# Hybrid mLSTM and sparse-attention block: the opening by token tiles with the first half of mv, and another rate for top-k

## The chip, the core and the metric

The kernel runs on one NeuronCore of a Trainium2 chip. The metric is the time of one execution on the device in microseconds (us). One profiled execution, with a trace of every engine, stands beside the timed runs. TensorE (PE in the rows) multiplies, VectorE (DVE), ScalarE (ACT) and GpSimd (POOL) work on rows, SyncE (SP) issues most transfers.

## What is computed

One decoder block on 512 tokens of width 1024, all in float32: an RMS norm, one wide input projection, an mLSTM group and a sparse attention group side by side, an output projection, and a gated per-layer embedding with a final norm. Cut to what matters here:

```python
u = rmsnorm(h, norm_in[i])
proj = u @ w_in[i]
(m_q, m_k, m_v, m_o, m_z, m_if, a_q, a_k, a_v, a_z,
 ix_q, ix_k, ix_w) = jnp.split(proj, SPLIT_POINTS, axis=-1)
qk = jax.nn.silu(causal_dwconv(jnp.concatenate([m_q, m_k], axis=-1), conv_w[i]))
...
hm = mlstm_chunkwise(mq, mk, m_v, log_i, log_f)
hm = jax.nn.sigmoid(m_o) * norm(hm) * jax.nn.silu(m_z)
# sparse attention: score[t, s] = sum_h ix_w[t, h] * relu(ix_q[t, h] . ix_k[s]), causal,
# each token attends to its 128 best keys, softmax with a relative bias
ha = dsa_attention(a_q, a_k, a_v, ix_q, ix_k, ix_w, rel_bias) * jax.nn.silu(a_z)
h = h + jnp.concatenate([hm, ha], axis=-1) @ w_out[i]
h = h + (p[i] @ w_ple[i]) * jax.nn.sigmoid(h @ w_ple_gate[i])
return rmsnorm(h, norm_final)
```

## The kernel before

Every large product is made in three passes of a reduced float32: each operand is split into a high part (wh, uH: a copy by ScalarE) and a low part (wl, uL: a subtraction by VectorE, or by GpSimd for the slabs in `POOLP`), and TensorE adds high times high, high times low and low times high. u, the normalised input, lies in SBUF with its 1024 features over the partitions, in 8 pieces of 128 (kt), as uH and uL. Weights come in slabs of 512 KB (raw, 3 buffers; wh and wl, 4 each), in the order of a plan; `piece()` gives the next slab and has the later ones loaded and split.

The projection goes in blocks of 512 columns: `dense_fm` gives features by tokens, `dense_tm` tokens by features. Both use four PSUM banks (tag mm), and the next block may begin in a bank when the one before it has been evacuated. Four more banks (tag x) serve transposes and small products. The order is: opening with iq (the indexer's queries) and misc (its keys, its weights and the gates), mq, mk, mv in two halves, then o and z, then mLSTM woven with the second o and z, av and two pairs of aqk, then attention woven with the rest, the output projection and the gate.

Beside the blocks runs a queue of small steps, `back`: the 24 score steps of the indexer, the gate sequences, the conv of the eight mq and mk pieces, and 48 top-k steps (16 rounds of MAX and MATCH_REPLACE for three token tiles), later `split_mix`, the split of the mLSTM's result (mixH, mixL). `beat()`, called twice per slab row of a block, gives the queue one credit; a step costs COST_SC, COST_CV, COST_TK or COST_MX. So the costs set how densely the steps are spread over the blocks. What is left of top-k is issued ahead of attention. From the order of the program and its own model of time the scheduler sets each engine's order; the opening alone is written out by hand (`manual_schedule`).

In the opening before, the eight x transfers come first. For each token tile ScalarE squares the two halves of x (`junk`), the sum goes to the power of -0.5 on GpSimd; TensorE transposes x by pieces of 128 features and spreads the four rows of factors over the partitions (`rps`, then `rB`). Per kt VectorE then scales 512 tokens at once (`scaled`), ScalarE and VectorE split (`high`, `low`), one half slab of iq weights is split (`weights`), and TensorE adds that kt's products to the four iq banks. misc follows from a transfer of its own (`mraw`). The rest of the text calls the eviction of mv by its rows: v (high, ScalarE; low, VectorE); that of z: sz. The relative bias goes out to memory and back: `tdram` is written and `tz` read, both issued from ScalarE's queue, so ScalarE stands until the write has landed.

Of the kernel before, what the change touches and what calls it, by code (L numbers as in the profile page):

```python
# [32 lines left out]
COST_SC, COST_CV, COST_TK, COST_MX, RATE = 1.3, 1.5, 1.5, 3.0, 1.4  # L33
# [14 lines left out]
def block_kernel(ctx: ExitStack, tc: tile.TileContext, x, p, w_in, b_gate, conv_w, w_out, norm_in,  # L48
# [94 lines left out]
    def split(k):  # L143
        raw = loaded.pop(k)
        nk, n = raw.shape[1:]
        h = wp.tile([P, KP * S], F32R, tag="wh", bufs=NW, name="wh")[:, 0:nk * n].rearrange("p (k n) -> p k n", n=n)
# [3 lines left out]
        ready[k] = h, l  # L150

# [109 lines left out]

# [41 lines left out]
    def weights(kt):

        q, k = kt // KP, kt % KP
        if k == 0:
            iqw[q] = [wp.tile([P, KP, S], F32R, tag=t, bufs=NW, name=t) for t in ("wh", "wl")]
        h, l = iqw[q]
        A.activation(h[:, k, :], loaded[q][:, k, :], AF.Copy)
        (G if kt in POOLW else V).tensor_tensor(l[:, k, :], loaded[q][:, k, :], f(h)[:, k, :], OP.subtract)  # L310

    us = {}

    def scaled(kt):
        us[kt] = tmp("u")
        V.scalar_tensor_tensor(us[kt], xt[kt], g_in(kt), rB, op0=OP.mult, op1=OP.mult)

    def high(kt):
        A.activation(uH[:, kt, :], us[kt], AF.Copy)

    def low(kt):
        V.tensor_tensor(uL[:, kt, :], us.pop(kt), f(uH[:, kt, :]), OP.subtract)

    load(0)
    load(1)
    EN = mybir.EngineType
    with tc.manual_schedule(engines={EN.PE, EN.DVE, EN.Activation, EN.Pool}):

        for kt in range(4):
            xt[kt] = mm_bank(f"xt{kt}")  # L330
        vps = x_bank("vps")
        xt[4], xt[5] = x_bank("xt4"), x_bank("xt5")
        rps = x_bank("rps")
        for i in range(NT):
            if i == 3:
                T.transpose(vps[:, 0:48], vrows, ident[0:48, 0:48])
                V.tensor_copy(vcols[:, 0:48], vps[:, 0:48])
                V.tensor_scalar(vcols[:, 48:56], vcols[:, 8:16], 0.25, None, op0=OP.mult)
            for kt in range(4):
                turn(kt, i)  # L340
            for c in range(2):
                junk = tmp("junk")
                A.activation(junk, xs[i][c], AF.Square, scale=D ** -0.5, accum_out=ss[:, i, c:c + 1])
            V.scalar_tensor_tensor(ss[:, i, 2:3], ss[:, i, 0:1], EPS, ss[:, i, 1:2], op0=OP.add, op1=OP.add)
            G.tensor_tensor(ss[:, i, 3:4], ss[:, i, 2:3], neghalf[:, 0:1], OP.pow)
        for i in range(3):
            spread(i)
        weights(0)
        turn(4, 0)
        turn(4, 1)  # L350
        turn(4, 2)
        spread(3)
        turn(4, 3)
        for i in range(NT):
            turn(5, i)
        rB = tmp("rB")
        A.activation(rB, rps, AF.Copy)
        xt[6] = x_bank("xt6")
        for i in range(NT):
            turn(6, i)  # L360
        for kt in range(KT):
            if kt == 0:
                scaled(0)
                scaled(1)
            high(kt)
            low(kt)
            if kt < KT - 1:
                weights(kt + 1)
            if kt < KT - 2:
                scaled(kt + 2)  # L370
            if kt == 0:
                mraw = wp.tile([P, KT, 80], F32, tag="raw", bufs=NR, name="mraw")
                nc.sync.dma_start(mraw[:, :, 0:72], wv[:, :, C_IK:C_IK + 72])
                nc.sync.dma_start(mraw[:, :, 72:80], wv[:, :, C_IF:C_IF + 8])
                nc.sync.dma_start(gb[72:76, 0:1], b_gate[0, 0:4].rearrange("(h o) -> h o", o=1))
# [604 lines left out]
```

## Time and profile before

| | us |
|---|---|
| median of 3 runs | 527.07 (526.15 to 527.16) |
| the profiled execution's own time | 526.94 |
| its span, first to last instruction | 524.9 |
| TensorE busy | 498.6 (95%) |
| VectorE busy | 349.3 (67%) |
| ScalarE busy | 259.8 (49%) |
| GpSimd busy | 81.3 (15%) |

The span and what lies around it (2.0 us) make the execution's time. A busy TensorE is not TensorE at its peak: records of products overlap, and the distance from one start to the next is what one costs. The idle time of an engine counts only where the engine that ends last waits for it; so the waits of TensorE and the chain of work are read before any sum of busy time.

### The profile page before, as it was taken

What the parts mean: (1) busy time and instruction counts of PE and PEld (TensorE: products, weight loads), DVE (VectorE), ACT (ScalarE), POOL (GpSimd) and SP (SyncE); (2) the same over time, 40 slices, a digit from 0 to 9 for tenths busy, and PEclk for the clock granted to TensorE, in tenths of its full rate; (3) what the DMA queues carried; (4) which work ended last, traced back from release to release, by engine and by line L of the source; (5) the groups of instructions that cost most, each with busy time, mean ns of one, the idle gap of its engine ahead of it and who ended that gap; (6) DMA issues with size and microseconds to landing.
All of it is one profiled execution on the core that took longest, in us unless ns stands there. A gap on an engine that the chain in (4) does not pass through costs nothing.

```text
span 524.9 us, 6706 instructions
## 1 busy us (share of the span) xinstructions
PE 498.6 (95%) x2370; PEld 409.3 (78%) x2370; DVE 349.3 (67%) x718; ACT 259.8 (49%) x518; POOL 81.3 (15%) x110
## 2 busy tenths in 40 slices
PE   4999999894999999999999999999999999999994
PEld 3887878683878888888888787888878888888884
DVE  0945287999999827355745759979887441452744
ACT  5636183763132425465545658767875321232533
POOL 4501022231111322310101012111111000000011
PEclk9999999997999999999999999999999999999998
DMA  8352557322223224223422312121123443213012
GB/s 264 108 181 84 104 87 172 117 82 81 81 85 116 82 81 140 77 92 112 131 81 90 102 61 76 46 81 74 47 82 121 161 160 113 88 41 120 1 51 109
DMA packets 37280, 52.24 MB, mean 100 GB/s; under 512 B 4156, under 2 KB 16732, under 8 KB 37248
## 3 DMA queue, kind: packets, MB, share of 16 engines
q1 hardware_dynamic: 30464, 42.34, 25.2%
q10 hardware_dynamic: 6688, 9.46, 7.3%
q8 instruction: 18, 0.29, 0.2%
q14 instruction: 14, 0.11, 0.1%
q0 software_dynamic: 96, 0.02, 0.0%
HBM read 48.13 MB, written 3.69 MB: 99 GB/s over the span
## 4 chain that ended last, share of the span: by engine, by line
PE 74%; DVE 12%; DMA 8%; ACT 2%; issue 2%; SPq 0%; POOL 0%; POOLq 0%; ACTq 0%; DVEq 0%
DMA tdram<-tv 7%; PE wo L233 4%; PE wo L232 4%; PE wo L234 4%; PE o L212 3%; PE z L212 3%; PE z L214 3%; PE o L213 3%; PE z L213 3%; PE o L214 3%; DVE mqk L450 2%; PE aqk L212 2%; PE aqk L213 2%; PE aqk L214 2%; PE mv L232 2%
## 5 line engine op out<-in xcount | busy, mean ns | idle before, releaser
L148 ACT ACTIVATE wh<-raw 128x1024 fp32r<-128x1024 f32 x70 | 74.0, 1058 | 110.6 <-PE wo L234 36.5
L149 DVE TENSOR_TENSOR wl<-raw,wh 128x1024 fp32r<-128x1024 f32 x56 | 68.6, 1225 | 68.5 <-ACT wh L148 68.3
L149 POOL TENSOR_TENSOR wl<-raw,wh 128x1024 fp32r<-128x1024 f32 x14 | 33.8, 2415 | 134.8 <-ACT wh L148 123.4
L232 PE MATMUL wo<-wh,mixH 128*128 128x512 f32 x96 | 38.9, 405 | 0.1
L234 PE MATMUL wo<-wh,mixL 128*128 128x512 f32 x96 | 37.9, 395 | 0.0
L233 PE MATMUL wo<-wl,mixH 128*128 128x512 f32 x96 | 37.9, 395 | 0.0
L232 PE MATMUL mv<-wh,uH 128*128 128x512 f32 x64 | 26.2, 410 | 8.5 <-DVE v L546 6.6
L212 PE MATMUL aqk<-uH,wh 128*128 128x512 f32 x64 | 26.4, 413 | 0.0
L234 PE MATMUL mv<-wh,uL 128*128 128x512 f32 x64 | 26.0, 406 | 0.0
L525 DVE MATCH_REPLACE8 sc<-m,sc 128x256 f32<-128x256 f32 (+2 forms) x48 | 25.8, 544 | 0.0
L212 PE MATMUL o<-uH,wh 128*128 128x512 f32 x64 | 25.8, 402 | 0.0
L212 PE MATMUL z<-uH,wh 128*128 128x512 f32 x64 | 25.7, 402 | 0.0
L233 PE MATMUL mv<-wl,uH 128*128 128x512 f32 x64 | 25.7, 401 | 0.0
L214 PE MATMUL aqk<-uH,wl 128*128 128x512 f32 x64 | 25.4, 397 | 0.0
L214 PE MATMUL z<-uH,wl 128*128 128x512 f32 x64 | 25.4, 396 | 0.0
L213 PE MATMUL o<-uL,wh 128*128 128x512 f32 x64 | 25.4, 396 | 0.0
L214 PE MATMUL o<-uH,wl 128*128 128x512 f32 x64 | 25.3, 396 | 0.0
L213 PE MATMUL z<-uL,wh 128*128 128x512 f32 x64 | 25.3, 396 | 0.0
L213 PE MATMUL aqk<-uL,wh 128*128 128x512 f32 x64 | 25.3, 395 | 0.0
L524 DVE MAX8 m<-sc 128x8 f32<-128x256 f32 (+2 forms) x48 | 24.8, 550 | 0.2 <-POOL sc L516 0.2
L731 POOL TENSOR_SCALAR bm<-sc,tz 128x128 f32<-128x128 f32 (+1 forms) x16 | 13.7, 857 | 71.3 <-DVE ha L772 21.2
L514 DVE SCALAR_TENSOR_TENSOR sc<-relu,iwt,sc 128x256 f32<-128x256 f32 (+2 forms) x21 | 14.2, 676 | 13.7 <-ACT relu L509 12.9
(245 smaller groups left out, 1363.6 us busy)
## 6 DMA issues: line engine op xcount, KB each, us to landing
raw<-in_w_in_dram SPq DMA_DIRECT2D x44, 512.0 KB, 3.4
raw<-in_w_out_dram SPq DMA_DIRECT2D x12, 512.0 KB, 3.5
raw<-in_w_in_dram SPq DMA_DIRECT2D x16, 256.0 KB, 2.9
raw<-in_w_ple_gate_dram SPq DMA_DIRECT2D x8, 512.0 KB, 3.5
x<-in_x_dram SPq DMA_DIRECT2D x8, 256.0 KB, 5.7
xr<-in_x_dram ACTq DMA_DIRECT2D x2, 1024.0 KB, 5.6
tdram<-tv ACTq DMA_DIRECT2D x1, 1536.0 KB
tz<-tdram ACTq DMA_DIRECT2D x1, 1024.0 KB, 6.3
```

The source lines that it names most:

```text
L148: A.activation(h, raw, AF.Copy)
L149: (G if k in POOLP else V).tensor_tensor(l, raw, f(h), OP.subtract)
L212: T.matmul(banks[b][:, 0:nt], h[:, k, bs], uH[:, kt, tok0:], start=(kt == 0), stop=False)
L213: T.matmul(banks[b][:, 0:nt], h[:, k, bs], uL[:, kt, tok0:], start=False, stop=False)
L214: T.matmul(banks[b][:, 0:nt], l[:, k, bs], uH[:, kt, tok0:], start=False, stop=(kt == KT - 1))
L232: T.matmul(banks[i], aH(kt, i), h[:, k, :], start=first, stop=False)
L233: T.matmul(banks[i], aH(kt, i), l[:, k, :], start=False, stop=False)
L234: T.matmul(banks[i], aL(kt, i), h[:, k, :], start=False, stop=last)
L514: V.scalar_tensor_tensor(sc, r, w, sc, op0=OP.mult, op1=OP.add)
L524: V.max(out=m8, in_=sel[i])
L525: V.match_replace(out=sel[i], in_to_replace=m8, in_values=sel[i], imm_value=-3e38)
L731: G.tensor_scalar(bm[:, 0:n - 256], sel[i][:, 0:n - 256], tz[:, h, 0:1], None, op0=OP.add)
```

## The change

The opening now goes by token tiles of 128. norm_in is loaded as one row (`grow`) and spread over the partitions by two products with a column of ones (`gB`), in full float32. For each tile the squares are shared between ScalarE and VectorE, x is scaled in place, transposed, split, and multiplied at once by the first half of mv (`values(i, q)`: tile i, slab q). x and the weight slabs are loaded in turn, and all eight low weight parts of the opening are GpSimd's. iq and misc follow as ordinary blocks, misc as a slab of its own, so every later slab moves by one place against `POOLP`; only mv's second half stays between mk and o. The cost of a conv step goes from 1.5 to 2.2 and that of a top-k step from 1.5 to 2.4.

```diff
-COST_SC, COST_CV, COST_TK, COST_MX, RATE = 1.3, 1.5, 1.5, 3.0, 1.4
+COST_SC, COST_CV, COST_TK, COST_MX, RATE = 1.3, 2.2, 2.4, 3.0, 1.4
...
-                nc.sync.dma_start(xs[i][c], x[0, i * P:(i + 1) * P, c * S:(c + 1) * S])
...
+        nc.gpsimd.dma_start(grow, norm_in)
+        nc.gpsimd.dma_start(vrows[0:8, :], m_norm[0].rearrange("(k p) -> k p", p=P))
...
+    def load_x(i):
+        for c in range(2):
+            nc.sync.dma_start(xs[i][c], x[0, i * P:(i + 1) * P, c * S:(c + 1) * S])
...
+    def split_misc(raw):
...
-    for cols in ([(C_IQ, S)], [(C_MQ, S)], [(C_MK, S)], [(C_MV, S)], [(C_MV + S, S)], [(C_MO, S)], [(C_MZ, S)],
+    MISC = [(C_IK, IDH + IH), (C_IF, 2 * MH)]
+    for cols in ([(C_MV, S)], [(C_IQ, S)], MISC, [(C_MQ, S)], [(C_MK, S)], [(C_MV + S, S)], [(C_MO, S)], [(C_MZ, S)],
...
+    def squares(i):
+        junk = [tmp(f"junk{c}") for c in range(2)]
+        A.activation(junk[0], xs[i][0], AF.Square, scale=D ** -0.5, accum_out=ss[:, i, 0:1])
+        V.tensor_tensor_reduce(junk[1], xs[i][1], xs[i][1], 1.0 / D, EPS, OP.mult, OP.add, ss[:, i, 1:2])
+        V.tensor_tensor(ss[:, i, 2:3], ss[:, i, 0:1], ss[:, i, 1:2], OP.add)
+        G.tensor_tensor(ss[:, i, 3:4], ss[:, i, 2:3], neghalf[:, 0:1], OP.pow)
+
+    def scaled(i):
+        for c in range(2):
+            V.scalar_tensor_tensor(xs[i][c], xs[i][c], ss[:, i, 3:4], gB[c], op0=OP.mult, op1=OP.mult)
...
+    def turn(i):
+        for c in range(2):
+            xt[i, c] = x_bank(f"xt{i}_{c}", (P, 4, P))
+            for k in range(4):
+                T.transpose(xt[i, c][:, k, :], xs[i][c][:, k * P:(k + 1) * P], ident)
+
+    def high(i):
+        for c in range(2):
+            A.activation(uH[:, 4 * c:4 * c + 4, i * P:(i + 1) * P], xt[i, c], AF.Copy)
+
+    def low(i):
+        for c in range(2):
+            d = (slice(None), slice(4 * c, 4 * c + 4), slice(i * P, (i + 1) * P))
+            V.tensor_tensor(uL[d], xt[i, c], f(uH[d]), OP.subtract)
+
+    def weights(q):
+        h, l = w0[q] = [wp.tile([P, KP, S], F32R, tag=t, bufs=NW, name=t) for t in ("wh", "wl")]
+        for k in range(KP):
+            A.activation(h[:, k, :], loaded[q][:, k, :], AF.Copy)
+            G.tensor_tensor(l[:, k, :], loaded[q][:, k, :], f(h)[:, k, :], OP.subtract)
+
+    def values(i, q):
+        h, l = w0[q]
+        for k in range(KP):
+            kt = KP * q + k
+            T.matmul(mvb[i], u_h(kt, i), h[:, k, :], start=(kt == 0), stop=False)
+            T.matmul(mvb[i], u_l(kt, i), h[:, k, :], start=False, stop=False)
+            T.matmul(mvb[i], u_h(kt, i), l[:, k, :], start=False, stop=(kt == KT - 1))
...
+    for i in range(NT):
+        load_x(i)
+        if i < NR:
+            load(i)
+    with tc.manual_schedule(engines={EN.PE, EN.DVE, EN.Activation, EN.Pool}):
+        for c in range(2):
+            T.matmul(gB[c], one, grow[:, c * S:(c + 1) * S], start=True, stop=True)
+        squares(0)
+        scaled(0)
+        turn(0)
+        weights(0)
+        high(0)
+        squares(1)
+        low(0)
+        scaled(1)
+        values(0, 0)
+        turn(1)
...
+        turn(3)
+        high(3)
+        low(3)
+        weights(3)
...
+        for i in range(NT):
+            for q in range(NT):
+                if i == 3 or q == 3:
+                    values(i, q)
+            evac0(i, mvb[i])
...
+    run(dense_fm(4, evac_iq, tok0=P, name="iq"))
+    mh, ml = piece()
...
-    for c in range(2):
-        run(dense_tm(u_h, u_l, list(range(KT)), evac_mv(c), name="mv"))
+    run(dense_tm(u_h, u_l, list(range(KT)), evac_mv(1), name="mv"))
```

Three places show what moves. The first is the opening, on VectorE: before, for each kt a scaling (u), a low part (uL) and a low weight part (wl).

```order
L316 SCALAR_TENSOR_TENSOR u<-xt_115,vcols,rB 128x512 [waits PE_49]
L322 TENSOR_TENSOR uL<-u,uH 128x512 [waits Activation_49]
L310 TENSOR_TENSOR wl<-raw,wh 128x512 [waits DMAHW7_49,Activation_49]
L316 SCALAR_TENSOR_TENSOR u<-xt_116,vcols,rB 128x512 [waits PE_49]
L322 TENSOR_TENSOR uL<-u,uH 128x512 [waits Activation_49]
```

Now, behind the first tile: ISA rows on junk are the squares' second half and its read, the row on ss is the sum with ScalarE's half, then the low parts of tile 0 and the scaling of tile 1.

```order
L302 ISA junk_150,ss<-x_1_72 128x512 [waits DMAHW4_49]
L302 ISA ss 128x1
L303 TENSOR_TENSOR ss<-ss 128x1 [waits DVE_49,Activation_49]
L325 TENSOR_TENSOR uL<-xt_0_131,uH 128x4x128 [waits PE_49]
L325 TENSOR_TENSOR uL<-xt_1_136,uH 128x4x128 [waits PE_49]
L308 SCALAR_TENSOR_TENSOR x_0_71<-x_0_71,ss,gB_99 128x512 [waits DMAHW3_49,Pool_49]
L308 SCALAR_TENSOR_TENSOR x_1_72<-x_1_72,ss,gB_100 128x512
```

On ScalarE there, now: the square of tile 0, two weight copies, the high parts of tile 0, the square of tile 1.

```order
L301 ACTIVATE junk_123,ss<-x_0_69 128x512 [waits DMAHW0_49]
L330 ACTIVATE wh<-raw 128x512 [waits DMAHW2_49]
L330 ACTIVATE wh<-raw 128x512
L320 ACTIVATE uH<-xt_0_131 128x4x128 [waits PE_49]
L320 ACTIVATE uH<-xt_1_136 128x4x128 [waits PE_49]
L301 ACTIVATE junk_149,ss<-x_0_71 128x512 [waits DMAHW3_49]
L330 ACTIVATE wh<-raw 128x512 [waits DMAHW5_49]
```

The low parts of tile 0 stand behind the sum of tile 1, and that needs a square that stands on ScalarE behind weight copies and the high parts of tile 0.

The second place is VectorE at the end of the mv block that follows mk, with the last rows ahead of v. Before (mv's first half; sc are the score tiles of top-k):

```order
L453 SCALAR_TENSOR_TENSOR mqk_881<-raw_882,mqk_881 128x512 [waits Activation_49]
L524 MAX m_3_1320<-sc_742 128x8 [waits DVE_49]
L525 MATCH_REPLACE sc_468<-m_1_1335,sc_468 128x256
L525 MATCH_REPLACE sc_742<-m_3_1320,sc_742 128x512 [waits DVE_49]
L546 TENSOR_TENSOR v_0_0_1027<-mv_891,v_0_0_1026 128x2x256 [waits DMAHW3_49,Activation_49]
```

And now (mv's second half):

```order
L466 SCALAR_TENSOR_TENSOR mqk_1021<-raw_1022,mqk_1021 128x512 [waits Activation_49]
L538 MATCH_REPLACE sc_608<-m_1_1540,sc_608 128x256
L537 MAX m_2_1599<-sc_732 128x8
L149 TENSOR_TENSOR wl<-raw,wh 128x1024 [waits DMAHW6_49,Activation_49]
L291 TENSOR_TENSOR v_0_1_1164<-mv_1031,v_0_1_1163 128x2x256 [waits Activation_49]
```

From the first conv row on, seven MAX and seven MATCH_REPLACE rows stood ahead of this v before, and now five and four; one wl row more and (some rows ahead, not shown) two qkL rows of the mLSTM have come before it.

The third is VectorE at the end of z, where sz evacuates its four banks. Before, top-k ends ahead of z's eviction:

```order
L528 TENSOR_SCALAR sc_742<-sc_742 128x512 [waits DVE_49]
L149 TENSOR_TENSOR wl<-raw,wh 128x1024 [waits DMAHW6_49,PE_49,Activation_49]
L581 SCALAR_TENSOR_TENSOR sz<-sz,z_1438 128x512 [waits Activation_49]
L582 SCALAR_TENSOR_TENSOR go_1403<-go_1403,sz 128x512 [waits DVE_49]
```

Now sz stands among top-k rows, and the last rounds follow behind:

```order
L538 MATCH_REPLACE sc_882<-m_3_2812,sc_882 128x512 [waits DVE_49]
L149 TENSOR_TENSOR wl<-raw,wh 128x1024 [waits DMAHW7_49,PE_49,Activation_49]
L578 SCALAR_TENSOR_TENSOR sz<-sz,z_1384 128x512 [waits Activation_49]
L537 MAX m_1_2815<-sc_608 128x8
L578 SCALAR_TENSOR_TENSOR sz<-sz,z_1385 128x512 [waits Activation_49]
L579 SCALAR_TENSOR_TENSOR go_1353<-go_1353,sz 128x512 [waits DVE_49]
L579 SCALAR_TENSOR_TENSOR go_1361<-go_1361,sz 128x512 [waits DVE_49]
L578 SCALAR_TENSOR_TENSOR sz<-sz,z_1386 128x512 [waits Activation_49]
L538 MATCH_REPLACE sc_608<-m_1_2815,sc_608 128x256
L579 SCALAR_TENSOR_TENSOR go_1371<-go_1371,sz 128x512 [waits DVE_49]
```

The eight split_mix steps, queued behind top-k, move with it: before, six of the mixL rows stand among those of mLSTM and two among those of attention; now all eight stand among those of attention.

## Rows read from the trace of the kernel before

**Rows 1.** Page, part 1: busy time, share, instructions of TensorE.
```profile
PE 498.6 (95%) x2370; PEld 409.3 (78%) x2370; DVE 349.3 (67%) x718; ACT 259.8 (49%) x518; POOL 81.3 (15%) x110
```

**Rows 2.** Waits of TensorE, whole span: total us, times, longest.
```profile
PE mv L232 <- DVE v L546: 6.6, 1, 6.6
...
PE mv L232 <- ACT mqk L463: 1.9, 2, 1.6
```

**Rows 3.** Chain of work, 0 to 60 us: start, us, what.
```profile
21.77 0.44 PE xt L297 x4
...
39.75 0.23 PE mq L212
...
49.98 0.95 PE tv_ps L430 x2
```

**Rows 4.** Timeline, 0 to 26 us: start, us, engine, line, operation.
```profile
5.86 0.56 POOL L345 TENSOR_TENSOR ss<-ss,neghalf 128x1 f32<-128x1 f32 x1 [1.94 <-DVE ss L344]
...
7.80 0.63 ACT L343 ACTIVATE junk<-x 128x512 f32<-128x512 f32 x1
...
12.14 0.63 ACT L309 ACTIVATE wh<-raw 128x512 fp32r<-128x512 f32 x1 [0.57 <-DMA raw<-in_w_in_dram]
...
12.50 1.93 PEld L297 LDWEIGHTS xt<-ident,x 128*128 128x128 f32 x9
...
12.85 1.27 POOL L310 TENSOR_TENSOR wl<-raw,wh 128x512 fp32r<-128x512 f32 x1 [0.46 <-ACT wh L309]
...
15.09 0.69 DVE L322 TENSOR_TENSOR uL<-u,uH 128x512 fp32r<-128x512 f32 x1
```

**Rows 5.** DMA issues, 0 to 60 us: count, size, median us to landing.
```profile
vrows<-in_norm_in_dram POOLq DMA_DIRECT2D x1, 4.0 KB, 3.7
```

**Rows 6.** Windows: busy time by engine, granted clock, DMA share, GB/s.
```profile
10.00:15.00 5.00, 4.83 (x22) 4.15 (x21) 1.96 (x6) 3.36 (x10) 2.37 (x3) 1.00 0.72 200
...
128.00:130.00 2.00, 1.70 (x4) 1.41 (x5) 2.00 (x6) 1.23 (x2) 0.26 (x1) 0.50 0.28 67
...
320.00:340.00 20.00, 19.35 (x100) 15.69 (x99) 19.39 (x51) 17.18 (x38) 3.22 (x4) 1.00 0.19 54
```

**Rows 7.** Timelines of ScalarE (first two) and VectorE, 51 to 128 us.
```profile
51.41 1.30 ACTq L436 DMA_DIRECT2D tdram<-tv  x1
...
87.98 0.41 ACTq L440 DMA_DIRECT2D tz<-tdram  x1
...
69.09 2.12 DVE L450 SCALAR_TENSOR_TENSOR mqk<-raw,vcols,mqk 128x511 f32<-128x511 f32 x1 [0.67 <-ACT mqk L463]
...
78.95 2.89 DVE L450 SCALAR_TENSOR_TENSOR mqk<-raw,vcols,mqk 128x510 f32<-128x510 f32 x1
...
89.13 0.75 DVE L514 SCALAR_TENSOR_TENSOR sc<-relu,iwt,sc 128x512 f32<-128x512 f32 x1 [2.75 <-ACT relu L509]
...
127.57 0.68 DVE L546 TENSOR_TENSOR v<-mv,v 128x512 fp32r<-128x512 f32 x1
```

**Rows 8.** Timeline of TensorE at the block borders.
```profile
128.31 0.79 PE L232 MATMUL mv<-wh,uH 128*128 128x512 f32 x1 [6.57 <-DVE v L546]
...
131.03 0.46 PE L232 MATMUL mv<-wh,uH 128*128 128x512 f32 x1
...
198.56 0.39 PE L212 MATMUL o<-uH,wh 128*128 128x512 f32 x1
```

**Rows 9.** Page, part 5, VectorE: group, count, busy us, mean ns, idle before.
```profile
L149 DVE TENSOR_TENSOR wl<-raw,wh 128x1024 fp32r<-128x1024 f32 x56 | 68.6, 1225 | 68.5 <-ACT wh L148 68.3
...
L525 DVE MATCH_REPLACE8 sc<-m,sc 128x256 f32<-128x256 f32 (+2 forms) x48 | 25.8, 544 | 0.0
...
L524 DVE MAX8 m<-sc 128x8 f32<-128x256 f32 (+2 forms) x48 | 24.8, 550 | 0.2 <-POOL sc L516 0.2
```

**Rows 10.** Timeline of VectorE: the first sz row and a mixL row.
```profile
194.48 0.69 DVE L581 SCALAR_TENSOR_TENSOR sz<-sz,z 128x512 f32<-128x512 f32 x1 [5.58 <-ACT sz L580]
...
320.12 0.69 DVE L596 TENSOR_TENSOR mixL<-go,mixH 128x512 fp32r<-128x512 f32 x1
```

More of the change, by code (lines that the diff above doesn't have):

```diff
@@ L150, in split @@
         ready[k] = h, l
+    def split_misc(raw):
+        h = wp.tile([P, KT, NM], F32R, tag="wh", bufs=NW, name="mh")
+        l = wp.tile([P, KT, NM], F32R, tag="wl", bufs=NW, name="ml")
+        for t in (h, l):
+            G.memset(f(t)[:, :, 76:104], 0.0)
+        for a, b, n in ((0, 0, 76), (104, 76, 4)):
+            A.activation(h[:, :, a:a + n], raw[:, :, b:b + n], AF.Copy)
+            V.tensor_tensor(l[:, :, a:a + n], raw[:, :, b:b + n], f(h)[:, :, a:a + n], OP.subtract)
+        return h, l
     def feed(k):
@@ new lines, in values @@
+    def values(i, q):
[5 more added lines that the diff above has]
+            T.matmul(mvb[i], u_h(kt, i), l[:, k, :], start=False, stop=(kt == KT - 1))
+    evac0 = evac_mv(0)
+    EN = mybir.EngineType
+    for i in range(NT):
[15 more added lines that the diff above has]
+        turn(1)
+        weights(1)
+        high(1)
+        squares(2)
+        low(1)
+        scaled(2)
+        values(0, 1)
+        values(1, 0)
+        values(1, 1)
+        turn(2)
+        load(3)
+        weights(2)
+        high(2)
+        squares(3)
+        low(2)
+        scaled(3)
+        for i in range(3):
+            for q in range(3):
+                if i == 2 or q == 2:
+                    values(i, q)
[3 more added lines that the diff above has]
+        weights(3)
+        vps = x_bank("vps")
+        T.transpose(vps[:, 0:40], vrows, ident[0:40, 0:40])
+        V.tensor_copy(vcols[:, 0:40], vps[:, 0:40])
+        V.tensor_scalar(vcols[:, 40:48], vcols[:, 0:8], 0.25, None, op0=OP.mult)
+        for i in range(NT):
+            for q in range(NT):
+                if i == 3 or q == 3:
+                    values(i, q)
+            evac0(i, mvb[i])
@@ L271, in evac_iq @@
+    for q in range(4):
+        loaded.pop(q)
+    nc.sync.dma_start(gb[72:76, 0:1], b_gate[0, 0:4].rearrange("(h o) -> h o", o=1))
+    nc.sync.dma_start(gb[104:108, 0:1], b_gate[0, 4:8].rearrange("(h o) -> h o", o=1))
+    count[:] = [4, 4, 4]
+    feed(3)
+    qi = {}
     def evac_iq(b, ps):
@@ L303, in weights @@
[L303 to L375, printed above, removed]
-                nc.sync.dma_start(gb[104:108, 0:1], b_gate[0, 4:8].rearrange("(h o) -> h o", o=1))
-                load(2)
-                load(3)
-            if kt == 3:
-                mh = wp.tile([P, KT, NM], F32R, tag="wh", bufs=NW, name="mh")
-                ml = wp.tile([P, KT, NM], F32R, tag="wl", bufs=NW, name="ml")
-                G.memset(f(mh)[:, :, 76:104], 0.0)
-                G.memset(f(ml)[:, :, 76:104], 0.0)
-                for a, b, n in ((0, 0, 76), (104, 76, 4)):
-                    A.activation(mh[:, :, a:a + n], mraw[:, :, b:b + n], AF.Copy)
-                    G.tensor_tensor(ml[:, :, a:a + n], mraw[:, :, b:b + n], f(mh)[:, :, a:a + n], OP.subtract)
-            for b in range(min(kt + 1, 4)):
-                for k in range(kt if b < kt or kt >= 4 else 0, kt + 1):
-                    iq_step(b, k)
-            if kt == 2:
-                xt[7] = x_bank("xt7")
-                for i in range(NT):
-                    turn(7, i)
-            if kt == 5:
-                mps = x_bank("mps")
-                for k in range(6):
-                    misc_step(k)
-        misc_step(6)
-        misc_step(7)
@@ L401, in block_kernel @@
-    for q in range(4):
-        loaded.pop(q)
-    count[:] = [4, 4, 4]
-    feed(3)
-    for b in range(4):
-        evac_iq(b, iqp[b])
+    run(dense_fm(4, evac_iq, tok0=P, name="iq"))
+    mh, ml = piece()
+    mps = x_bank("mps")
+    for kt in range(KT):
+        T.matmul(mps[0:NM, :], mh[:, kt, :], uH[:, kt, :], start=(kt == 0), stop=False)
+        T.matmul(mps[0:NM, :], mh[:, kt, :], uL[:, kt, :], start=False, stop=False)
+        T.matmul(mps[0:NM, :], ml[:, kt, :], uH[:, kt, :], start=False, stop=(kt == KT - 1))
```

70 lines of the change are left out of this document (28 added, 42 removed).

## The prediction

> **What bounds the kernel now.** I read the page first: TensorE is busy 498.6 of 524.9 us [rows 1], so the time is its matmul stream plus its idle time, and a change pays only where TensorE waits. The list of its waits, longest first, shows one large one behind the opening, 6.6 us for VectorE's v rows (line 546), and two of 1.9 together at the start of mv [rows 2]; all else of weight lies in the opening. The chain of work there shows the products of mq from 39.75 on [rows 3]. I call mq's first matmul M (39.6, where the record of that row begins; the chain counts its end part). Up to M, TensorE has 96 iq matmuls of 0.173 and 24 misc matmuls of 0.233 (22.2 us together), some 37 transposes and small products of 0.11 (4 us): 13 us of the first 39.6 are idle. One product of 128x512 takes 0.233, a block of 96 of them 22.4 us [rows 3].
>
> **The opening (term A).** It now ends with the 96 products of mv's first half done, and iq and misc (22.2) follow. So I walk to the end of that block, E, and compare E + 22.2 with 39.6 + 22.4 = 62.0 of before. The walk, queue by queue, each wait taken in the order that the order rows show:
>
> - norm_in is issued by GpSimd at 1.25 and lands 3.7 later [rows 5], at 4.95. The two products that spread it over 128 partitions are full fp32 like tv_ps, 0.95 each [rows 3]; transposes up to 14.6 went at 0.21, later ones at 0.11 [rows 3, 4], so I give these two double, to 6.9 and 8.7.
> - The square, sum and power of token tile 0 end where they did, at 6.4 (5.86 + 0.56) [rows 4]. Scaling (0.7 each) ends at 7.7 and 9.4, the second half held by the second fp32 product.
> - The first raw weights are now the third issue, with the bytes ahead of them that x tile 1 closes in before; that tile was in use by 7.80 [rows 4]. Before, they came at 12.14 [rows 4]. ScalarE's two wh copies stand ahead of its uH copies and end at 9.05, the uH copies at 9.95 and 10.7, the square of tile 1 (0.63 and a read of 0.19) at 11.45.
> - VectorE has the sum of tile 1 ahead of the uL rows of tile 0. So these start at 11.65 and end (0.69 each, [rows 4]) at 12.35 and 12.95: TensorE stands after its first product at 10 until 12.4.
> - From there tile 1 repeats the chain: scaled 14.3, turned 14.85, uH 15.55, square of tile 2 16.3, uL 17.15. The products of (1,0) and (1,1) end at 19.8, tile 2 is turned at 20.7, and TensorE then has 30 products and 8 transposes, to 28.6.
> - weights(3) stands last: wh after uH of tile 3, 30.0 and 30.5; GpSimd's two wl rows, 1.27 each [rows 4], end at 31.3 and 32.6. TensorE waits for them (3 us idle) and then has 36 products: E = 41.3.
>
> E + 22.2 = 63.5 against 62.0: **A = +1.5 us**. The first product comes 5 us earlier than before (there iq began beside the first uL row, 15.09 [rows 4]), but the block is fed by a chain that goes tile after tile through four engines. Bounds: the double price of the fp32 products and all GpSimd rows at the pace beside them gives +3.5; the raw slab a microsecond early and the fp32 products at full pace, -0.5.
>
> **mq to the second o block (term C).** The order of TensorE from mq on is as before, but for two things: only one mv block stands between mk and o, and the score products start after 19 mq products, not 40. VectorE's queue from the first conv row to the first v row is nearly the same list. In before it ran from 69.09 to 127.57 [rows 7], 58.5 us, of which 3.1 idle (2.75 of it at 89.13, when ScalarE stood in its queue until 87.98 for the tdram write issued at 51.41 [rows 7]). The new order has 5 MAX and 4 MATCH_REPLACE there, not 7 and 7, one more wl row and two qkL rows: by 0.55, 0.54 and 0.08 for the load, 1.2, 0.6 [rows 9] that is -2.9 + 1.2 + 1.2 = -0.5. The tdram write is issued 4.9 us earlier against the mq stream, so its wait no longer starves VectorE: the 3.1 go. First conv row: M + 28.9 (69.09 - 39.6 = 29.5, less 0.6 of small waits at mq's start). First v row: M + 28.9 + 54.9 = M + 83.8, in before M + 88.0. TensorE had the mv block done 6.6 before 128.31 [rows 8], at M + 82.1; less the 1.9 at mv's start (which ScalarE owed to the same late chain) and the 0.6 that is M + 79.6. So with v's own 0.7 a wait of 5 us is left of the 6.6. It again lets the clock fall: the granted clock was 0.50, the 1.2 GHz level, at 128 to 130 [rows 6], and the six products from 128.31 to 131.03 took 2.72 and not 1.4 us [rows 8]; I keep the 1.2.
>
> Behind it VectorE has less room than it had. Before, it had mv's second half, o and z (67 us) for the 16 top-k rounds and was idle 5.6 us right ahead of the first sz row [rows 10]. Now o and z alone, 45.8 us. Its rows up to the first sz row: 14 of 16 rounds less what is done, 42.1 - 4.2 = 37.9 (a round of three pairs at 3.0 us: the records of 48 pairs are 50.6 us [rows 9], and they overlap by a twentieth); three v, four wl, two qkL, gcol, 7.9: together 45.8. TensorE needs 44.9 + 0.7 + the 1.2 of the slow clock = 46.9 until it wants that bank. It fits by half a microsecond. So the second o block starts 46.9 after the restart at M + 84.5: with M = 63.5 at 194.9, where before it started at 198.56 [rows 8]. **A and C together: -3.6 us.**
>
> **Attention (term D).** The split_mix steps now stand behind a slower top-k and land in the attention stage: eight mixL there, before two. VectorE is busy 19.39 of 20 us at 320 to 340 [rows 6]; two of the six new rows fall into that stretch, 0.6 each [rows 10], with as many mixH copies on ScalarE; the other four fall later, where there is room. From 0 (all covered) to 3.6 (none); I take **D = +1.0**.
>
> The rest is at nothing: after attention the order is row for row the same; the misc loads with their short rows leave the opening; GpSimd has 13 weight rows after the opening, not 14, and that one lands on VectorE in mlstm, where it is two fifths idle.
>
> **The sum**: -3.6 + 1.0 = -2.6. The profiled run took 526.94, the median is 527.07. **526.9 - 2.6 = 524.3.** Own range by the bounds of A, D and half of C's idle: 521.5 to 527.5.
>
> **The rivals.**
> - The wait at the end of mv vanishes. Four rows there took 2.1 to 2.9 us beside a GpSimd weight row and not 0.74 (two of them in [rows 7]), 7 us in all; the weight rows shift by one slab, and if none meets a conv row, v comes in time, the wait falls to about 1 us and the clock stays up: -3.5 more, 520.8. For: the shift. Against: four GpSimd rows still lie in the stretch.
> - The opening packs densely: E = 35.6 if TensorE never waits after its first product, 518.6. Against: ScalarE's and VectorE's queues above. Chance small.
> - VectorE comes late (the other side). From the first conv row to the first sz row it has 101 us with half a microsecond spare. If the 3.1 of idle stay and two weight rows on GpSimd block it in o and z as at 69.09 and 78.95 (1.4 and 2.2 [rows 7]), TensorE gets 6.2 more: 530.5. It decides from 3.6 on. For: no slack is left; before had 5.6. Against: MAX and MATCH_REPLACE were not stretched at 128 to 182.
> - The clock is low through the first tiles. The granted clock reads 1.00 at 10 to 15 [rows 6], yet nine transposes from 12.50 took 1.93 us, 0.21 each, and those at 21.77 0.11 [rows 3, 4], as at half pace. If tile 0 and 1 run so, six products and eight transposes on the chain cost 2 us more: 526.4. By the Trainium skill, page "TensorE: Matmul & The Clock Gate", section Part 1, "the default state is throttled, and activity releases the throttle": by that rule the sparse start speaks for this rival, the clock row against it.
> - That it does not do what it says: the top-k rate could move no row. The order rows show that it does (two rounds end behind z), so no chance.
>
> **How the numbers follow.** Forecast 0.39 (0.31 faster, 0.08 same); wait gone 0.14, faster; dense opening 0.08, faster; low clock 0.14 (0.04 faster, 0.10 same); VectorE late 0.25 (0.23 slower, 0.02 same). Against a bound of 0.2%, about what a measurement of this kernel can tell from no change: faster 0.57, same 0.20, slower 0.23. Range: from the dense opening to the price of a late VectorE, 518.6 to 530.5; half of each of those two lies outside, some 0.17.
>
> **What would show it.** The first mv product near 10 and a gap of 2 us behind it; mv's last one near 41; a gap near 29 to 32 that ends with GpSimd's wl; the wait for v before o at about 5 us, with the granted clock down behind it; sz not waiting for ScalarE; the second o block at 195. It is wrong if mq starts before 61 or after 66, if the wait before o is under 2 or over 8, or if a new wait of over 2 us stands between z and the second o block or in attention.

## The result, and the profile after

The changed kernel takes 536.05 us (median of 6 runs, 533.11 to 538.19), the kernel before beside it 527.32: the ratio is 1.0171, 95% interval 1.0149 to 1.0193. The forecast was 524.3, with a range of 518.6 to 530.5. It is wrong in sign, and the time lies outside the range.

The spans of the two profiled executions are 524.9 and 535.2; the one of the changed kernel is the longest of its six (the others: 531.3 to 534.7), so the stretches below explain more than the 8.7 between the medians. The starts of TensorE's blocks show where the 10.3 came in (the mv block that moved ahead of mq, 22.4, is added to mq's start in before, as in the prediction):

| stretch | before | after | change | predicted |
|---|---|---|---|---|
| to mq's first product | 62.0 | 67.4 | +5.4 | +1.5 |
| mq to z's first product | 113.4 | 113.3 | -0.1 | -5.1 |
| z to the second o block | 23.2 | 23.2 | 0 | 0 |
| second o block to av | 57.6 | 61.3 | +3.7 | 0 |
| av to the first logits | 57.5 | 57.5 | 0 | 0 |
| first logits to wo | 65.7 | 66.5 | +0.9 | +1.0 |
| wo to the end | 145.6 | 146.0 | +0.4 | 0 |

TensorE's waits in the changed kernel (total us, times, longest; compare [rows 2]):

```profile
PE o L224 <- DVE v L291: 7.1, 1, 7.1
PE gB L349 <- DMA grow<-in_norm_in_dram: 5.4, 1, 5.4
PE hp_ps L611 <- ACT hm L663: 1.9, 1, 1.9
PE mv L338 <- DVE uL L325: 1.7, 2, 1.5
PE mk L224 <- ACT mqk L476: 1.2, 1, 1.2
PE mv L337 <- ACT wh L330: 1.1, 1, 1.1
PE mv L339 <- POOL wl L331: 0.9, 2, 0.6
PE mv L244 <- ACT mqk L476: 0.7, 2, 0.4
```

The wait for v did not get shorter (7.1, before 6.6), and a wait of 1.9 for hp_ps, in the mLSTM stage, is new. In front, 5.4 is the start, when there is nothing to do yet; 1.5, 1.1 and 0.9 are the gaps of the opening.

**The opening.** TensorE's timeline (start, us, what, idle before and its releaser):

```profile
10.89 0.79 PE L337 MATMUL mv<-wh,uH 128*128 128x512 f32 x1
13.20 0.79 PE L338 MATMUL mv<-wh,uL 128*128 128x512 f32 x1 [1.52 <-DVE uL L325]
...
14.22 0.63 PE L337 MATMUL mv<-wh,uH 128*128 128x512 f32 x1
14.64 0.63 PE L338 MATMUL mv<-wh,uL 128*128 128x512 f32 x1
...
22.17 1.03 PE L316 MATMUL xt<-ident,x 128*128 128x128 f32 x8
...
32.33 0.50 PE L337 MATMUL mv<-wh,uH 128*128 128x512 f32 x1 [1.07 <-ACT wh L330]
...
34.92 0.80 PE L339 MATMUL mv<-wl,uH 128*128 128x512 f32 x1 [0.27 <-POOL wl L331]
35.51 0.63 PE L337 MATMUL mv<-wh,uH 128*128 128x512 f32 x1
...
45.20 0.34 PE L224 MATMUL iq<-uH,wh 128*128 128x384 f32 x1
```

The walk has its stations: a first product at 10.9 (forecast 10), a gap behind it, tile 2 turned from 22.2 on (forecast 19.8), a gap that ends with the low parts of slab 3. What it lacks is the pace. The products from 13.8 to 15.5 are 0.43 apart and not 0.23, and behind the gap at 32 to 35 they are so again. The windows (last columns: granted clock, DMA share, GB/s) show the second of the two, and not the first (the last section says why):

```profile
13.00:16.00 3.00, 2.80 (x8) 2.21 (x9) 3.00 (x5) 0.39 (x1) 2.67 (x3) 1.00 0.37 134
...
34.00:36.00 2.00, 1.73 (x6) 1.08 (x5) 0.00 (x0) 0.24 (x1) 1.13 (x9) 0.73 0.07 6
36.00:38.00 2.00, 2.00 (x6) 1.61 (x5) 0.69 (x1) 0.35 (x1) 0.00 (x0) 0.50 0.77 256
38.00:40.00 2.00, 2.00 (x9) 1.61 (x8) 0.69 (x1) 0.80 (x2) 0.00 (x0) 0.92 0.00 0
```

**mq to o.** First VectorE's timeline:

```profile
104.62 1.22 DVE L149 TENSOR_TENSOR wl<-raw,wh 128x1024 fp32r<-128x1024 f32 x1
105.76 2.77 DVE L527 SCALAR_TENSOR_TENSOR sc<-relu,iwt,sc 128x384 f32<-128x384 f32 x1
...
133.73 2.90 DVE L466 SCALAR_TENSOR_TENSOR mqk<-raw,mqk 128x512 f32<-128x512 f32 x1
...
139.42 3.31 DVE L495 TENSOR_TENSOR_SCAN rows<-rows,rows 12x512 f32<-12x512 f32 x1
...
154.88 0.68 DVE L291 TENSOR_TENSOR v<-mv,v 128x512 fp32r<-128x512 f32 x1
...
156.01 0.68 DVE L291 TENSOR_TENSOR v<-mv,v 128x512 fp32r<-128x512 f32 x1
```

GpSimd's timeline at the same times:

```profile
104.13 3.97 POOL L149 TENSOR_TENSOR wl<-raw,wh 128x1024 fp32r<-128x1024 f32 x1 [5.43 <-ACT wh L148]
...
133.24 2.84 POOL L149 TENSOR_TENSOR wl<-raw,wh 128x1024 fp32r<-128x1024 f32 x1
...
139.04 2.61 POOL L149 TENSOR_TENSOR wl<-raw,wh 128x1024 fp32r<-128x1024 f32 x1 [2.70 <-ACT wh L148]
155.69 2.38 POOL L149 TENSOR_TENSOR wl<-raw,wh 128x1024 fp32r<-128x1024 f32 x1 [14.04 <-ACT wh L148]
```

The three long rows (2.77, 2.90 and 3.31) take 0.61, 0.68 and 1.22 elsewhere. Each ends about its own length behind the GpSimd row beside it (133.24 + 2.84 = 136.1 and 133.73 + 2.90 = 136.6), as if it stood until that one is done. The v row at 156.01 takes its 0.68 beside a GpSimd row. With those at 96.43 and 113.63 five rows are stretched, by 1.4, 2.2, 2.2, 2.2 and 2.1, before rounding 10.0 us together. Before, there were four, 7.0 together (two of them in [rows 7]).

**The mLSTM stage.** Rows of VectorE, GpSimd and TensorE from 218 on:

```profile
218.10 2.99 POOL L149 TENSOR_TENSOR wl<-raw,wh 128x1024 fp32r<-128x1024 f32 x1 [8.89 <-ACT wh L148]
...
218.79 2.33 DVE L660 SCALAR_TENSOR_TENSOR st<-st,gcol 128x1 f32<-128x1 f32 x1
...
221.19 0.55 POOL L661 TENSOR_TENSOR st<-st,neghalf 128x1 f32<-128x1 f32 x1
...
222.30 0.44 PE L611 MATMUL hp_ps<-ident,hm 128*128 128x128 f32 x2 [1.95 <-ACT hm L663]
...
222.93 0.63 PE L225 MATMUL o<-uL,wh 128*128 128x512 f32 x1
```

A row of one element in each partition takes 2.33 us (0.21 for the next ones) and ends at 221.12, with GpSimd's row at 221.09. The power on GpSimd, the scaling on ScalarE and TensorE's transposes follow it; the granted clock is 0.50, the 1.2 GHz level, at 224 to 226, and eight products cost 0.2 each more. So one GpSimd row costs 1.9 + 1.6 = 3.5 of the 3.7 here. The kernel before has such a meeting too, with a later st row:

```profile
219.10 2.40 POOL L149 TENSOR_TENSOR wl<-raw,wh 128x1024 fp32r<-128x1024 f32 x1 [2.61 <-ACT wh L148]
219.74 1.77 DVE L663 SCALAR_TENSOR_TENSOR st<-st,gcol 128x1 f32<-128x1 f32 x1
```

There TensorE has no wait behind it. What counts is which row is held, and who waits for it.

### The profile page after: what moved, and what is told of

Read it like the earlier page. It is cut to its first block, busy times and chain, and to the rows that moved or that the text cites. A ratio compares the mean times of both kernels' runs of the same rounds, so it can differ in the third digit from the quotient of the medians.

```text
span 535.2 us, 6728 instructions
## 1 busy us (share of the span) xinstructions
PE 505.3 (94%) x2370; PEld 412.5 (77%) x2370; DVE 354.0 (66%) x724; ACT 257.2 (48%) x509; POOL 88.6 (17%) x113
## 4 chain that ended last, share of the span: by engine, by line
PE 69%; DVE 21%; ACT 5%; issue 2%; POOL 1%; DMA 1%; POOLq 0%; ACTq 0%; DVEq 0%
PE wo L245 4%; PE wo L244 4%; PE wo L246 4%; DVE sc L538 4%; DVE m L537 3%; DVE wl L149 2%; PE aqk L224 2%; PE aqk L225 2%; PE aqk L226 2%; PE mv L339 2%; PE mv L338 1%; PE wg L244 1%; DVE mqk L463 1%; PE z L224 1%; PE wg L245 1%
## 5 line engine op out<-in xcount | busy, mean ns | idle before, releaser
L149 DVE TENSOR_TENSOR wl<-raw,wh 128x1024 fp32r<-128x1024 f32 x57 | 69.8, 1225 | 71.7 <-ACT wh L148 71.3
L224 PE MATMUL o<-uH,wh 128*128 128x512 f32 x64 | 27.5, 430 | 7.1 <-DVE v L291 7.1
L225 PE MATMUL o<-uL,wh 128*128 128x512 f32 x64 | 27.0, 421 | 0.0
L226 PE MATMUL o<-uH,wl 128*128 128x512 f32 x64 | 26.8, 419 | 0.0
L527 DVE SCALAR_TENSOR_TENSOR sc<-relu,iwt,sc 128x256 f32<-128x256 f32 (+2 forms) x21 | 15.0, 714 | 15.1 <-ACT relu L522 14.8
L906 POOL TENSOR_TENSOR fs<-fs,neghalf 128x1 f32<-128x1 f32 x4 | 3.7, 932 | 119.1 <-DVE fs L905 119.1
L246 PEld LDWEIGHTS wo<-wh,mixL 128*128 128x128 f32 x96 | 18.0, 188 | 4.3
L244 PEld LDWEIGHTS wo<-wh,mixH 128*128 128x128 f32 x96 | 18.0, 188 | 4.0 <-DVE ak L710 0.4
```

The source lines that it names most:

```text
L224: T.matmul(banks[b][:, 0:nt], h[:, k, bs], uH[:, kt, tok0:], start=(kt == 0), stop=False)
L225: T.matmul(banks[b][:, 0:nt], h[:, k, bs], uL[:, kt, tok0:], start=False, stop=False)
L226: T.matmul(banks[b][:, 0:nt], l[:, k, bs], uH[:, kt, tok0:], start=False, stop=(kt == KT - 1))
L244: T.matmul(banks[i], aH(kt, i), h[:, k, :], start=first, stop=False)
L246: T.matmul(banks[i], aL(kt, i), h[:, k, :], start=False, stop=last)
L527: V.scalar_tensor_tensor(sc, r, w, sc, op0=OP.mult, op1=OP.add)
```

## The experiments

All the kernels below compute the whole block, as the kernel before does.

| run | median us | ratio to before, 95% |
|---|---|---|
| rates_back | 534.34 | 1.0148 (1.0120 to 1.0177) |
| before_new_rates | 527.35 | 1.0014 (0.9997 to 1.0031) |
| weights3_early | 531.10 | 1.0090 (1.0063 to 1.0117) |
| fill_opening | 534.90 | 1.0145 (1.0111 to 1.0179) |
| pool_shift | 531.75 | 1.0100 (1.0078 to 1.0123) |
| slab34_on_vector | 532.93 | 1.0116 (1.0088 to 1.0144) |
| no_pool_conv | 529.03 | 1.0044 (1.0024 to 1.0063) |
| before_no_pool_conv | 524.39 | 0.9949 (0.9924 to 0.9975) |
| fill_before_o | 541.73 | 1.0283 (1.0245 to 1.0321) |
| combined | 525.20 | 0.9966 (0.9949 to 0.9983) |
| combined_old_rates | 521.72 | 0.9893 (0.9872 to 0.9915) |
| combined_filled | 520.19 | 0.9880 (0.9858 to 0.9902) |

**The rates, undone in the changed kernel and alone in the kernel before.**

```diff
-COST_SC, COST_CV, COST_TK, COST_MX, RATE = 1.3, 2.2, 2.4, 3.0, 1.4
+COST_SC, COST_CV, COST_TK, COST_MX, RATE = 1.3, 1.5, 1.5, 3.0, 1.4
```

> The changed kernel with the old costs of a conv and a top-k step (1.5 and 1.5). My theory: the costs are worth about 1 us. The opening (mq at 67.4), VectorE's list from the first conv row to v and the wait for v before o (7.1) stay; only the mixL rows go back from attention into the mLSTM stage, and attention gives back its 0.9: 535.0. Rival A, the costs cause the loss: v comes late and the wait in the mLSTM stage arises because top-k still runs there; then the wait for hp_ps at 222 goes and the time falls below 531.

> The kernel before with the new costs (2.2 and 2.4) alone. My theory: within 1.5 us of the kernel before, 527 to 528.5: the wait for v at most 1 us shorter (one MAX and two MATCH_REPLACE fewer ahead of v, two qkL rows more), and up to 1 us more in attention for the mixL rows. Rival A, the costs cause the loss: 531 or more.

The waits for v (7.1) and hp_ps (2.0) stay, so rival A falls. From the first logits to wo it is 65.8 (66.5 in the changed kernel): the mixL rows are worth 0.7. Of the 2.5 by which the span is shorter (532.7) another 1.5 stem from the opening, whose code is the same: after the same gap at 32 to 35 the clock stayed at 1.00 in this execution (compare the window of 36 to 38 above):

```profile
36.00:38.00 2.00, 2.00 (x10) 1.64 (x9) 1.19 (x2) 0.67 (x2) 0.00 (x0) 1.00 0.84 254
```

In the kernel before the new rates cost nothing that can be told from no change, with 6.1 of wait for v.

**The fourth slab split early** (the call of `weights(3)` moves).

```diff
         scaled(3)
+        weights(3)
         for i in range(3):
...
         low(3)
-        weights(3)
```

> The changed kernel with the split of the fourth weight slab moved ahead of the products of tiles 0 to 2 with slab 2 (and so ahead of tile 3's high parts on ScalarE). My theory: the waits of 1.1, 0.6 and 0.3 at 32 to 35 go, the granted clock stays at 1.00 at 35 to 38 and gives back 1.7 there; mq starts at 63.7 in place of 67.4 and all behind it moves by as much: 532.3. Rival C, the opening's length is hidden later (VectorE sets the start of o): the wait before o grows by what the opening gives, 536.

Two windows behind the place of the gap:

```profile
33.00:35.00 2.00, 2.00 (x10) 1.60 (x9) 0.69 (x1) 1.19 (x2) 0.00 (x0) 1.00 0.00 0
35.00:37.00 2.00, 2.00 (x11) 1.59 (x9) 0.98 (x2) 1.06 (x1) 0.00 (x0) 1.00 0.00 0
```

TensorE is busy throughout and the granted clock is 1.00. From the turn of tile 3 to the end of the mv block it takes 11.1 and not 15.2 us. mq starts at 62.0 and not 67.4; of those 5.4 us 4.1 are this stretch, and 0.9 are that norm_in landed at 4.5 here and not at 5.4. The wait before o is 7.1 as it was, so nothing of it came back (rival C falls).

**A filler in the opening.** 8 transposes of the identity ahead of gB, 8 behind the first product.

```diff
+        for k in range(8):
+            T.transpose(mvb[3][:, 0:P], ident, ident)
...
+            if i == kt == 0:
+                for _ in range(8):
+                    T.transpose(mvb[3][:, 0:P], ident, ident)
```

> The changed kernel with 8 transposes of the identity ahead of the products that spread norm_in, and 8 behind the first mv product, where TensorE waits for the low parts of tile 0 (into the bank of tile 3, which starts later). My theory: the first products and transposes go at half pace because TensorE had been idle; with the filler the first tile's products take 0.23 each from the second product on (0.43 without) and the second tile is turned in 0.9 and not 1.6: mq starts some 2 us earlier, 534. Rival E, the pace in the first 17 us doesn't depend on what TensorE did before: mq at 67.4 as in the changed kernel, 536.

TensorE's timeline:

```profile
13.66 0.50 PE L341 MATMUL mv<-wh,uL 128*128 128x512 f32 x1 [0.22 <-DVE uL L325]
14.00 0.39 PE L342 MATMUL mv<-wl,uH 128*128 128x512 f32 x1
14.23 0.40 PE L337 MATMUL mv<-wh,uH 128*128 128x512 f32 x1
...
21.06 1.03 PE L316 MATMUL xt<-ident,x 128*128 128x128 f32 x8
```

The products are 0.23 apart from 14.0 on, and tile 2 is turned at 21.06 and not 22.17, though gB starts 0.4 later, behind the filler. So the pace does hang on what TensorE did before (rival E falls), while the time alone, whose interval overlaps that of the changed kernel, does not tell it. mq starts at 66.1, 1.3 earlier and not 2: the slow stretch behind the gap of slab 3 is there as before.

**GpSimd's slabs moved by one, and only slab 34 taken from it.**

```diff
-POOLP = range(8, 36, 2)
+POOLP = range(9, 37, 2)        # pool_shift
...
+POOLP = range(8, 34, 2)        # slab34_on_vector
```

> The changed kernel with GpSimd's slabs moved by one (9, 11, ... 35), so that from mk on GpSimd has the same slabs as before the change. My theory: two of the losses are VectorE rows that stand still beside a GpSimd weight row. The one at 218.8 in the mLSTM stage (2.33 for a row of 0.2) goes, and with it the 1.9 of TensorE's wait and the slow products behind it, 3.7 together; from the first conv row to v some four rows are stretched in place of five, 2 to 3 less, and the wait before o falls to about 5. 529.5 to 532. Rival B, GpSimd's slabs don't matter and VectorE is simply full: 536, both waits stay.

> The changed kernel with one slab (34, the one whose GpSimd row ran at 218.1 in the mLSTM stage) given to VectorE, nothing else moved. My theory: the row of 128x1 that took 2.33 takes 0.2, TensorE's wait of 1.9 for hp_ps goes, the granted clock stays up there: 3.7 less, 532.3; opening, wait before o and attention as in the changed kernel. Rival F, VectorE is late there because it has just ended top-k: the wait stays or only moves by half a us, 535 to 536.

In pool_shift the same st row takes 0.21:

```profile
217.36 0.21 DVE L660 SCALAR_TENSOR_TENSOR st<-st,gcol 128x1 f32<-128x1 f32 x1
```

TensorE waits at most 0.3 for hp_ps, and from z to av it takes 80.7, not 84.4: the 3.7 are gone. The other half of what I expected failed: the wait before o is 7.4, since three rows are stretched by 2.1 each, a TENSOR_SCALAR row by 1.8, and VectorE is idle 2.1 once more behind ScalarE's queue. With slab 34 alone, 2.4 of the 3.7 are gone; a wait of 1.1 stays, because VectorE's own weight row now stands ahead of st. Both say that the place of one GpSimd row makes this loss; with slab 34 alone top-k ends as late against mq as it did (rival F falls).

**No GpSimd weight rows between conv and v**, in the changed kernel and in the kernel before.

```diff
-POOLP = range(8, 36, 2)
+POOLP = (10, 12, *range(24, 36, 2))    # no_pool_conv
...
+POOLP = (8, *range(18, 36, 2))         # before_no_pool_conv
```

> The changed kernel with the five weight slabs that GpSimd splits between the first conv row and v (14 to 22) given to VectorE. My theory: the rows of VectorE that stand still beside a GpSimd weight row (five, 10.0 us more than the same rows elsewhere) go, five weight rows of 1.22 come: v 3.9 earlier against mq, the wait before o falls from 7.1 to about 3, and the slow products behind it (2.5 us) go in part: 529.5 to 532. Rival B, the help of GpSimd is worth its price and VectorE is only fuller: v is not earlier, 536 or more.

> The kernel before with the four weight slabs that GpSimd splits between the first conv row and v (10 to 16) given to VectorE. My theory: four rows there are stretched by 7.0 together; they go, four weight rows of 1.22 come: v 2.1 earlier, the wait before v falls from 6.6 to 4.5, with up to 1.2 from the clock: 524 to 525. Rival B: 527 or more.

VectorE's timeline in no_pool_conv:

```profile
133.76 1.22 DVE L495 TENSOR_TENSOR_SCAN rows<-rows,rows 12x512 f32<-12x512 f32 x1
...
147.35 0.68 DVE L291 TENSOR_TENSOR v<-mv,v 128x512 fp32r<-128x512 f32 x1
```

TensorE's waits there:

```profile
PE hp_ps L611 <- ACT hm L663: 2.4, 1, 2.4
...
PE o L224 <- DVE sz L578: 1.4, 1, 1.4
PE o L224 <- DVE v L291: 1.2, 1, 1.2
```

The scan that took 3.31 takes 1.22, and v comes 80.0 behind mq and not 87.5. That is more than the 3.9 I worked out: the order changed too and has no top-k row ahead of v any more (nine there in the changed kernel, 4.9 us with their loads). By the rows' sums the stretch from conv to v lost 10.0 and 4.9 and got 4.8 of weight rows and 3.0 of idle time; it shrank by 8.0. So two things made v early, and only the first is the one I meant to test. The wait is 1.2, the clock stays at 1.00, and z starts 10.0 earlier. Then VectorE, which still has its top-k to do, is late for sz and in mLSTM: av starts 7.5 earlier. This is the prediction's VectorE rival, seen once TensorE was ahead. The kernel before gains too: v at 84.9 behind mq (88.0), a wait of 4.8, and a time under both kernels. There five top-k rows still stand ahead of v, and not fourteen.

**A filler ahead of o.**

```diff
+    fill = x_bank("fill")
+    for k in range(56):
+        T.transpose(fill[:, 0:P], ident, ident)
```

> The changed kernel with 56 transposes of the identity (into a spare bank, read by nobody) between the gates' transposes and the o block, in TensorE's wait for v. My theory: the granted clock is still 1.00 when o starts, the first 12 products of o take 0.23 each and not 0.43, and 2.5 us come back: 533.5. Rival D, the slow start of o is not the clock's doing, or the 56 transposes hold o up: 536 or more.

Two windows of it (the columns as above):

```profile
150.00:154.00 4.00, 3.46 (x32) 3.22 (x30) 4.00 (x9) 4.00 (x7) 0.00 (x0) 1.00 0.24 90
154.00:158.00 4.00, 3.68 (x16) 3.00 (x17) 4.00 (x12) 0.30 (x1) 2.41 (x1) 1.00 0.50 136
```

And the longest of TensorE's waits:

```profile
PE o L224 <- DVE sz L581: 8.2, 1, 8.2
```

The price of the clock is confirmed: it stays at 1.00, and o takes 22.6 to z, not 25.1. The transposes do not hold o up either (rival D): it starts 88.1 behind mq, without them 88.2. But the kernel is 5.7 slower. The order has 43 MAX and 44 MATCH_REPLACE rows between v and the first sz, not 37 and 38, so sz comes 8.2 late. That the scheduler's model counts the filler as time of TensorE, and so finds room for them, is my reading and not shown. My theory had no word on that.

**A version that beats both.** The early fourth slab, no GpSimd weight rows from conv to v, and six slabs in a row on GpSimd during top-k; then the same with the old rates; then with the opening's filler.

```diff
-POOLP = range(8, 36, 2)
+POOLP = (10, 12, *range(24, 30))
```

> The changed kernel with three edits: the fourth slab split early (as in the run that did this alone), no GpSimd weight rows between the first conv row and v, and all six slabs from 24 to 29 on GpSimd, where VectorE is in top-k, whose rows were not stretched beside GpSimd. My theory: the parts add up: 536 less 4 for the opening (mq at 63 or less), less 7.7 for v, less the 1.4 for sz and 2.4 for hp_ps that VectorE was late by when v came early (three weight rows of 1.2 fewer in top-k): 520.5 to 523, under the kernel before. Rival B2: VectorE's total work from conv to the end of top-k sets the end, and what the opening gives comes back as waits for sz and hp_ps: 525 to 528.

> The same with the old costs of a conv and a top-k step (1.5 and 1.5). My theory: 0.5 to 1 us less than the combined one, from the mixL rows that go back from attention into the mLSTM stage; no change from conv to v. Rival A: nothing, or more by the mixL rows in mLSTM, which stand ahead of rows that TensorE waits for.

> The combined kernel with the old rates and the filler of the opening (8 transposes of the identity ahead of the products that spread norm_in and 8 behind the first mv product, as in the run that did this alone). My theory: tile 2 is turned 1.1 us earlier as it was there, and nothing behind the opening moves: 520.6. Rival G: a later start of a block makes other VectorE rows meet GpSimd's weight rows (as two did in the combined kernel with the new rates, 3.5 us), and the gain is lost or turned into 1 to 3 us more.

Two VectorE rows of the combined kernel:

```profile
148.02 1.96 DVE L560 TENSOR_SCALAR gcol<-gcol 128x16 f32<-128x16 f32 x1
...
174.19 2.49 DVE L603 TENSOR_TENSOR qkL<-mqk,qkH 128x512 fp32r<-128x512 f32 x1
```

the GpSimd rows beside them

```profile
147.54 2.41 POOL L149 TENSOR_TENSOR wl<-raw,wh 128x1024 fp32r<-128x1024 f32 x1 [24.56 <-ACT wh L148]
...
173.58 2.55 POOL L149 TENSOR_TENSOR wl<-raw,wh 128x1024 fp32r<-128x1024 f32 x1 [3.21 <-ACT wh L148]
```

and the first VectorE row with the old rates:

```profile
147.06 0.30 DVE L560 TENSOR_SCALAR gcol<-gcol 128x16 f32<-128x16 f32 x1
```

The combined kernel misses its 520.5 to 523 by two more such meetings: 1.7 and 1.8 us, behind which sz is late (2.9 of wait). The time and the wait are where rival B2 put them, but VectorE's total work is not the cause: with either rates 39 MAX and 38 MATCH_REPLACE rows stand between v and the first sz row, which take 48.8 us in the combined kernel and 45.3 with the old rates, and the two held rows are that difference. With the old rates the first of them meets only the last 0.1 us of a GpSimd row and the second none, the wait for sz is 0.3, and the time is 521.72: 3.5 less, where I had expected up to 1, and 1.1% under the kernel before. The filler on top (520.19) can't be told from that one; both profiled spans are 518.1. That its forecast of 520.6 came so close is luck: mq starts only 0.4 earlier, o takes 1.5 more to z at a fallen clock, and from the second o block to av it takes 1.2 less.

## Why the prediction was wrong, point by point

- **M and the bound.** Right: TensorE is busy 94% and its idle places are the places of the loss.
- **Term A, +1.5, measured +5.4; it failed.** The walk through the four engines held to within a microsecond as far as the first gap: first product 10.9 (10), gap 1.5 to 13.2 (12.4). From there it has the right order and the wrong pace: GpSimd's last rows end at 33.6 and 34.9 (31.3 and 32.6), and the block at 45.2 (41.3). Of the 3.9 missed, 0.9 stood there at the first product already (norm_in landed at 5.4, not 4.95; the scaling followed). 1.4 came from there to GpSimd's last rows, by the half pace of tile 0's products and tile 1's transposes, and 1.6 is the half pace behind the gap of slab 3. I had the first as a rival (2 us) with 0.14; its rows were in [rows 3, 4], and I let the granted clock of 1.00 in [rows 6] speak against it, which was no measurement (last section). The second I priced for the wait before o and not for a gap that I had forecast myself. By the Trainium skill, page "TensorE: Matmul & The Clock Gate", section Part 1, throttled is the default state; the pace of the first products agrees (0.43 apart, 0.23 with a filler ahead).
- **Term C, conv to v, forecast 54.9, measured 58.45; it failed.** The list was counted rightly: VectorE's idle time there fell from 3.3 to 0.4 (I had 3.1 to nothing), and fewer top-k rows stand ahead. The step that failed is that the rest of the list costs what it cost: the stretched rows grew from 7.0 to 10.0. The prediction knew of these rows, but only in a rival that let them vanish and in one that put two more into o and z; that a shift by one slab could as well add one here, it did not weigh. The rows show these 3.0 directly; no_pool_conv, where they are gone and v comes 7.4 earlier, agrees, though top-k rows left that stretch too. The shape is that of the Trainium skill, page "SBUF — State Buffer", section "Who interferes with whom": a VectorE instruction with two inputs in SBUF contends with a GpSimd instruction that reads SBUF, for a pair of ports that is an exclusive lock; TENSOR_SCALAR can contend too, in a mode with two ports. The traces agree: the stretched rows are rows with two SBUF inputs, and TENSOR_SCALAR from SBUF to SBUF (1.96 for 0.30), and they end with the GpSimd row or about their own length behind it; MAX, MATCH_REPLACE and the v rows, whose one input lies in PSUM, take their 0.4 to 0.7 beside one.
- **The wait before o, forecast 5, and the 1.2 of the clock.** 7.1 and 2.5: twelve products at half pace, not six. With the 3.6 of v, the 1.3 more of the clock make the 5.0 that this stretch missed. The wait grew less than v's delay because TensorE itself came there 81.1 behind mq and not 79.6; that costs nothing while v comes later still.
- **"It fits by half a microsecond", o and z.** Right: sz stands without a wait of TensorE, and from z to the second o block is 23.2 in both.
- **The rest at nothing.** This failed in mLSTM: 3.7 there, 3.5 of it by one GpSimd row, that of slab 34. I had counted the GpSimd rows (13, not 14) and not looked at what they stand beside.
- **Term D, +1.0.** Measured +0.9; rates_back gives 0.7 back.
- **The rivals.** The low clock came true in the opening. The late VectorE had the right mechanism in the wrong place: in the changed kernel conv, score, scan and st rows are held by GpSimd, and top-k in o and z is not. The range ended at 530.5 because it added no two of the cases, and three came at once.

## What to carry to other kernels

Where two engines shut each other out, a count of rows says little: list for each GpSimd row which VectorE row stands beside it and who waits for that one, and put GpSimd's rows where VectorE's rows have one SBUF input. Each gap that is forecast for TensorE can have a second price behind it, in products at half pace. A new start of the program moves all such meetings, so a forecast of a reordering needs a range that lets several of them go wrong together.

## What was not expected of the hardware

- The same gap does not always bring the clock down: behind identical waits at 32 to 35 us the granted clock fell to 0.50 in the changed kernel (1.6 us) and stayed at 1.00 in rates_back. Of the seven profiled executions that have this gap it fell in six. In combined_filled a wait of 1.2 before o was followed by 0.81 and 0.84 at 140 to 145 and 145 to 150; in combined_old_rates, without the filler, the same wait was not.
- The granted clock reads 1.00 at 13 to 16 us, where products stand 0.43 apart. The column counts 1.00 where the trace holds no record of the clock, and the first record stands only at 17.9 us in the changed kernel, where the products pass from 0.43 to 0.23, and at 15.1 in the kernel before. With the filler in the opening it stands at 12.9 and 13.4, in the other runs with the new opening at 15.5 to 19.2. So the 1.00 of [rows 6] at 10 to 15 says nothing, and ahead of the first record the distance of rows tells the pace.
- GpSimd is held as well: its row at 104.13 took 3.97 and not 2.4, beside a VectorE weight row.
